# Hybrid decoder layer on one core: conditioning sums spread over the projections, convolution halos on ACT, attention paced anew

## The chip, the cores and the metric

The kernel runs on one core of a Trainium2 chip. The core has a matrix engine (PE), a vector engine (DVE), a scalar engine (ACT), a general engine (POOL) and a queue engine (SP) that here issues the DMAs; each works through its own list of instructions in order. The metric is the device time of one execution in microseconds (us).

## The reference, cut to what matters

One decoder layer over 2048 tokens of width 1024, all in float32:

```python
mod = silu(c) @ w_ada + b_ada            # (1, 6*1024)
sh1, sc1, ga1, sh2, sc2, ga2 = jnp.split(mod, 6, axis=-1)
h  = rms_norm(x, g_attn) * (1 + sc1) + sh1
x  = x + ga1 * hybrid_mixer(h, ...)      # h @ w_in, two attentions, @ w_out
h2 = rms_norm(x, g_mlp) * (1 + sc2) + sh2
u  = causal_dwconv(h2 @ w_up, conv_w, conv_b)   # width 3 along the tokens
a, g = jnp.split(u, 2, axis=-1)
x  = x + ga2 * ((silu(g) * a) @ w_down)
y  = rms_norm(x, g_final)
```

Eight heads use attention over a sliding window of 128 tokens, eight use "forgetting" attention over all earlier tokens. `w_ada` has 1024 x 6144 numbers (24 MB); `mod` is one row, made by a product of a vector with that matrix.

## The kernel before

**Blocks and stages.** The tokens are cut into four blocks of 512 (n = 0 to 3). For each block there are three generators. `s1(n)` is the input projection. `s2(n)` is the attention. `s3(n)` is the output projection ("out", `L1179`), the row statistics, the up-projection (44 column blocks `ci` of 128 rows, 24 matmuls each, `L1297`) with the convolution, and the down-projection (`L1179` again). Every matmul operand is split into a high and a low float32r part (`wh`, `wl`; `hh`, `hl`; `ph`, `pl`), the high by ACT (`L384`, `L115`, `L724`), the low by DVE (`L385`, `L530`, `L725`), and each product is three matmuls.

**What sets the order.** `merge(main, side, ratio)` takes one event after another of a main generator and between them steps of an attention generator, so that the attention keeps to `ratio` times the main work that is done; `RM` scales these ratios. The five merges at the end of the function pair: s1(1) and s1(2) with s2(0); s3(0) with s2(1); s1(3) and s3(1) with s2(2); s3(2) with s2(3); s3(3) runs alone. An event `("B", us)` of the main generator is a place where PE would be idle, and attention may run there without main work. A scheduler then moves instructions by priority, on each engine, where their operands allow; what results is a fixed list per engine.

**Attention.** `s2` works on units. A unit of forgetting attention has scores (`L964`), which ACT copies out with a bias (`L981`), a column maximum (`L989`, `L991`), its spreading over rows (`L996`, `L1003`), a subtraction on DVE (`L1010`, `L1014`), the exponential on ACT (`L1015`), sums (`L1025`, `L1035`), and for each group of columns the split `ph`, `pl` (`L724`, `L725`) and the products with v (`L1059`, `L1062`). `DEPTH` is the number of split groups that are held before the oldest one's products are issued, `PB` the number of buffers for `ph` and for `pl`.

**Conditioning.** `w_ada` comes in 12 chunks of 512 columns, each in 8 steps of 256 KB. A step is one DMA (`wada`) and one DVE instruction (`L205` for the first of a chunk, `L207` for the others) that adds a scaled piece to `acc`; PE then sums `acc` over the partitions (`L262`, `L215`, `L226`). Chunks 0 to 3, which s1(0) needs, are made at the start in `first_groups`, whose DVE order is as written. Chunks 4 to 11 come from the generator `prologue_later`: 4 and 5 give the gate of the first residual (it must be there before s3(0)), 6 to 9 shift and scale of the second norm (`mod` at `L219`, `scl` at `L350`), 10 and 11 the second gate. `woven` takes one step of it after every eighth event of s1(1) and s1(2), and what the first gate lacks at their end in one go. `s3(0)` takes one step per event of its output projection, then in a loop (`while "mod" not in late`) whatever is missing up to `scl`, and two steps per pair of column blocks after that.

**The turn from out to up.** When the output projection of s3(n) ends, DVE forms the residual rows (`L1254`, `L1255`), ACT squares and sums them (`L491`), POOL takes the root (`L495`, `L496`), DVE and ACT scale the halves (`L1262`, `L1263`), PE transposes (`L517`), ACT applies `mod` and `scl` (`L525`, tile `hraw`) and splits (`L115`), DVE forms `hl` (`L530`), and the first up matmul can run.

**The convolution.** For each column block ACT evicts the PSUM tile `d` with bias and the third tap (`L1327`), DVE adds the other two taps (`L1330`, `L1333`). The first two columns of a block need the last two of the block before: `halo`. In blocks 1 to 3 DVE adds it (`L1338`); in blocks 0 to 2 ACT (`L1340`, two columns) and DVE (`L1341`, one column) form the halo for the next.

Of the kernel before, what the change touches and what calls it, by code (L numbers as in the profile page):

```python
# [11 lines left out]
AF = mybir.ActivationFunctionType  # L12
ALU = mybir.AluOpType
# [5 lines left out]
TB = 512  # L19
# [6 lines left out]
EPS = 1e-6  # L26
BIG = 1e30
NT = 10
RM = [1.0, 1.1, 1.0, 1.2]
GAPS = [1.5, 1.5, 1.2, 1.5]  # L30
FG = 3
NW = 1 + (FG > 0)
# [1 line left out]
FK = 4  # L34
WS = 10
KEEP = (0, 1)
DEPTH = 2
PB = 3
SD = 1
AD = 0  # L40
HOOKS = (13, 17, 20)
# [30 lines left out]
def tile_decoder_layer(  # L72
# [169 lines left out]
    def first_groups():  # L242
        rows = ready.pop(0)
        xts = []
        for k in range(KT):
            if k % 4 == 2:
                ps = pa.tile([P, 512], F32, tag="o", name="o0")
            else:
                ps = side_ps()
            transposes(ps, rows, k)  # L250
            xt = ap.tile([P, TB], F32, tag="act", name="xt")
            nc.scalar.copy(xt, ps)
            xts.append(xt)
        hh, hl = {}, {}
        acc = [dense_ps() for _ in range(4)]
        for tag, bufs in (("s", 3), ("o", 1), ("s", 3))[:FG]:
            acc.append(pa.tile([P, 512], F32, tag=tag, name="acc0", bufs=bufs))

        def shape(i, a):
            ps = side_ps(4)  # L260
            for j in range(4):
                nc.tensor.matmul(  # L262
                    ps[:, j : j + 1], a[:, j * P : (j + 1) * P], ones[:, 0:1],
                    start=True, stop=True,
                )
            js, jc = slice(2 * i, 2 * i + 2), slice(KT + 2 * i, KT + 2 * i + 2)
            nc.vector.tensor_add(mod[:, js], ps[:, 0:2], bada[:, js])
            nc.vector.tensor_add(mod[:, jc], ps[:, 2:4], bada[:, jc])
            nc.vector.scalar_tensor_tensor(
                scl[:, js], mod[:, jc], 1.0, gat[:, js], ALU.add, ALU.mult  # L270
            )

        def products(k, sets):
            a = k % 2
            for m in sets:
                i = NW * (k // 2) + m
                feed(i + 3, i + 2)
                wh, wl = parts[i]
                for g in range(4 * m, min(4 * m + 4, len(acc))):
                    gs = slice((g - 4 * m) * P, (g - 4 * m + 1) * P)  # L280
                    for j, (l, r) in enumerate(((wh, hh), (wh, hl), (wl, hh))):
                        nc.tensor.matmul(  # L282
                            acc[g], l[:, a, gs], r[k],
                            start=(k == 0 and j == 0), stop=(k == KT - 1 and j == 2),
                        )
                if a == 1:
                    parts.pop(i)
                    flow["used"] += 1

        prev = None  # L290
        for i in range(5):
            sums = None
            if i < 4:
                sums = ap.tile([P, 512], F32, tag="act", name="acc")
            for k in range(KT):
                if i < 4:
                    ada_pair(i, k, sums)
                if i > 0 and k == 1:
                    shape(i - 1, prev)
                    if i > 1:  # L300
                        for m in range(1, NW):
                            products(2 * i - 4, [m])
                            products(2 * i - 3, [m])
                if i > 0 and k in (3, 5):
                    kk = 2 * (i - 1) + (k - 3) // 2
                    modulate_one(*h_pair(hh, hl, kk), xts[kk], kk, 0, 0)
                    if k == 5:
                        products(kk - 1, [0])
                        products(kk, [0])
            prev = sums  # L310
            if i == 0:
                feed(3, 2)
        for m in range(1, NW):
            products(KT - 2, [m])
            products(KT - 1, [m])
        small_loads()
        for g in range(4):
            store_group(acc[g], q_d[0], 512 + g * P, 0.125)
        for g in range(FG):
            store_group(acc[4 + g], k_d[0], P + g * P, 1.0)  # L320
        return hh, hl
# [33 lines left out]
    def woven(side, extra, every):  # L355
        for i, event in enumerate(side):
            yield event
            if i % every == every - 1:
                next(extra, None)
        while "gate" not in late:  # L360
            next(extra)
# [170 lines left out]
    def h_pair(hh, hl, k, name="h"):  # L532
        if k not in hh:
            hh[k] = hp.tile([P, TB], F32R, tag="hh", name=name + "h")
            hl[k] = hp.tile([P, TB], F32R, tag="hl", name=name + "l")
        return hh[k], hl[k]
# [691 lines left out]
    def s3(n, after=()):  # L1228
# [58 lines left out]
        for f in range(NF):  # L1287
            if f == NF - 1:
                got[0, 0] = get(0)
                got[0, 1] = get(1)  # L1290
            res = []
            ups = []

            def up(ps, w, k, hf, hn):
                c = slice(hf * TB // hn, (hf + 1) * TB // hn)
                for i, (a, b) in enumerate(((0, h2h), (0, h2l), (1, h2h))):
                    nc.tensor.matmul(  # L1297
                        ps[:, c], w[a][:, k, :], b[k][:, c],
                        start=(k == 0 and i == 0), stop=(k == KT - 1 and i == 2),
                    )  # L1300

            if f == 0:
                ws = [weights(), weights()]
                ups = [dense_ps(), dense_ps()]
                for hf in range(2):
                    for part in range(2):
                        for k in range(KT):
                            need(k + 2, hf)
                            if hf == 0 and part == 1:
                                need(k // 2, 1)  # L1310
                            up(ups[part], ws[part], k, hf, 2)
                            if k % 4 == 3:
                                yield 1.3
            for part in range(2):
                ci = part * NF + f
                if f > 0:
                    w = weights()
                    ps = dense_ps()
                    for k in range(KT):
                        up(ps, w, k, 0, 1)  # L1320
                        if k % 2 == 1:
                            yield 1.3
                else:
                    ps = ups[part]
                u = tp.tile([P, TB], F32, tag="u", name="u", bufs=3)
                c0, c1, c2 = (cw[t][:, ci : ci + 1] for t in range(3))
                nc.scalar.activation(  # L1327
                    u, ps, AF.Identity, bias=cb[:, ci : ci + 1], scale=c2
                )
                nc.vector.scalar_tensor_tensor(  # L1330
                    u[:, 1:], ps[:, : TB - 1], c1, u[:, 1:], ALU.mult, ALU.add
                )
                nc.vector.scalar_tensor_tensor(  # L1333
                    u[:, 2:], ps[:, : TB - 2], c0, u[:, 2:], ALU.mult, ALU.add
                )
                hl = halo[:, ci, :]
                if n > 0:
                    nc.vector.tensor_add(u[:, 0:2], u[:, 0:2], hl)  # L1338
                if n < NB - 1:
                    nc.scalar.activation(hl, ps[:, TB - 2 : TB], AF.Copy, scale=c0)  # L1340
                    nc.vector.scalar_tensor_tensor(  # L1341
                        hl[:, 0:1], ps[:, TB - 1 : TB], c1, hl[:, 0:1], ALU.mult, ALU.add
                    )
                res.append(u)
            a, g = res
            for _ in range(2):
                next(extra, None)
            e = tp.tile([P, TB], F32, tag="t", name="e")
            nc.scalar.activation(e, g, AF.Tanh, scale=0.5)
            nc.vector.tensor_mul(a, a, g)  # L1350
            act = ap.tile([P, TB], F32, tag="act", name="act")
            nc.vector.scalar_tensor_tensor(act, e, 1.0, a, ALU.add, ALU.mult)
            acts.append(act)
# [101 lines left out]
    def chain(*gens):  # L1455
        for g in gens:
            yield from g
# [32 lines left out]
    def att_cost(n):  # L1490
        return MRG * (44.0, 72.0, 97.0, 124.0)[n]
# [20 lines left out]
    gat = columns(None, KT, "gat", g_raw)  # L1512
    late["extra"] = prologue_later()
    merge(s1(0), prologue_late(), 1.0)
    merge(woven(chain(s1(1), s1(2)), late["extra"], 8), s2(0), RM[0] * att_cost(0) / 190.0)
    merge(s3(0, [lambda: prime(2)]), s2(1), RM[1] * att_cost(1) / 383.0)
    merge(chain(s1(3), s3(1, [lambda: yprep(2, 1), lambda: prime(3)])), s2(2), RM[2] * att_cost(2) / 478.0)
    merge(s3(2, [lambda: yprep(3, 1)]), s2(3), RM[3] * att_cost(3) / 383.0)
# [73 lines left out]
```

## Time and profile before

| what | value |
|---|---|
| median of 3 runs | 2646.96 us (2644.52 to 2648.71) |
| the profiled execution's own time | 2648.82 us, its span 2647.1 us |
| PE, DVE, ACT busy | 96%, 73%, 55% of the span |
| HBM traffic over the span | 221 GB/s |
| chain that ended last, by engine | PE 83%, DVE 6%, DMA 6%, ACT 2% |

Busy time of PE counts matmuls that overlap, so it hides short waits; how fast PE really goes is read from how many matmuls end in a stretch, and from the granted clock (`PEclk`, 1.00 is full). Views "by window" give, for a stretch from A to B, its length, then for each engine busy time and the number of instructions, the clock, the DMA share and rate. The view of groups gives for each line the count, busy time, mean duration in ns, and the engine's idle time just before with what ended it.

### The profile page before, as it was taken

Reading aid. Unit: us, or ns where it says so; the run is one execution under the profiler, and the core shown is the slowest. Engines: PE = TensorE matmul, PEld = TensorE weight load, DVE = VectorE, ACT = ScalarE, POOL = GpSimd, SP = SyncE. Lnnn points to the kernel's source line nnn. Section 1 sums busy time; section 2 is a strip of 40 time slices with the busy share of each in tenths; the row PEclk is TensorE's granted clock in tenths of the full one; section 3 lists DMA queues with packets and bytes.
Section 4 is the critical chain, followed back from the end, with each engine's and each line's share of the span. In section 5 each row is a group of like instructions: output and inputs, shape, how many; then the busy total and the mean of one; then the engine's idle time right before and its main releaser. Section 6 shows DMA issues by size and latency. Waiting matters only on the chain.

```text
span 2647.1 us, 38431 instructions
## 1 busy us (share of the span) xinstructions
PE 2541.4 (96%) x12852; PEld 2151.1 (81%) x12852; DVE 1926.8 (73%) x3837; ACT 1458.4 (55%) x3061; POOL 84.1 (3%) x171
## 2 busy tenths in 40 slices
PE   7999999799999999999999999999998999999998
PEld 5888888688887889878888878888886778888887
DVE  6468767899998668788888767878888787444433
ACT  4456665555667675575556665755555666412222
POOL 0001000100000010000000001000000000000000
PEclk9999999799999999999999999999998999999999
DMA  6967679576556976756666799555544477655564
GB/s 230 305 203 254 204 231 344 182 254 211 188 189 212 288 239 215 251 199 240 228 230 235 258 290 312 176 182 194 187 153 148 139 235 246 252 191 191 193 238 173
DMA packets 304770, 588.25 MB, mean 222 GB/s; under 512 B 32188, under 2 KB 137396, under 8 KB 304572
## 3 DMA queue, kind: packets, MB, share of 16 engines
q1 hardware_dynamic: 304572, 585.79, 66.3%
q8 instruction: 102, 1.67, 0.3%
q14 instruction: 96, 0.79, 0.1%
HBM read 440.95 MB, written 144.71 MB: 221 GB/s over the span
## 4 chain that ended last, share of the span: by engine, by line
PE 83%; DVE 6%; DMA 6%; ACT 2%; issue 1%; SPq 1%; POOL 0%; POOLq 0%; DVEq 0%; ACTq 0%
PE d L1297 36%; PE d L1179 21%; PE d L619 8%; PE s L964 4%; PE d L647 3%; PE o L1062 2%; PE o L1059 2%; DVE t L1010 1%; DMA wada<-in_w_ada_dram 1%; PE d L282 1%; DMA q<-qd 1%; PE s L794 1%; PE mb L996 1%; PE pt L836 1%; DVE pl L725 1%
## 5 line engine op out<-in xcount | busy, mean ns | idle before, releaser
L1297 PE MATMUL d<-hh,wkh 128*128 128x512 f32 (+1 forms) x920 | 351.3, 384 | 3.3 <-ACT hh L115 1.6
L1297 PE MATMUL d<-hl,wkh 128*128 128x512 f32 (+1 forms) x920 | 353.2, 385 | 0.1
L1297 PE MATMUL d<-hh,wkl 128*128 128x512 f32 (+1 forms) x920 | 351.7, 383 | 0.0
L384 ACT CAST wh<-wr 128x1024 fp32r<-128x1024 f32 (+5 forms) x184 | 188.7, 1027 | 162.4 <-PE d L1297 72.0
L385 DVE TENSOR_TENSOR wl<-wr,wh 128x1024 fp32r<-128x1024 f32 (+5 forms) x184 | 219.0, 1191 | 80.0 <-ACT wh L384 78.4
L981 ACT ACTIVATE t<-s,bc 128x256 f32<-128x256 f32 (+3 forms) x464 | 201.1, 483 | 124.7 <-PE s L964 70.6
L1327 ACT ACTIVATE u<-d,cb,cw 128x512 f32<-128x512 f32 x176 | 136.3, 778 | 192.9 <-PE d L1297 179.8
L1330 DVE SCALAR_TENSOR_TENSOR u<-d,cw,u 128x511 f32<-128x511 f32 x176 | 130.4, 743 | 153.6 <-ACT u L1327 152.8
L724 ACT CAST ph<-t 128x512 fp32r<-128x512 f32 (+2 forms) x304 | 177.1, 591 | 110.0 <-PE o L1059 109.6
L1297 PE MATMUL d<-hh,wh 128*128 128x512 f32 (+1 forms) x552 | 211.1, 385 | 0.4 <-ACT hh L115 0.4
L1297 PE MATMUL d<-hh,wl 128*128 128x512 f32 (+1 forms) x552 | 211.0, 383 | 0.2 <-DVE wl L385 0.2
L1297 PE MATMUL d<-hl,wh 128*128 128x512 f32 (+1 forms) x552 | 211.0, 383 | 0.0
L725 DVE TENSOR_TENSOR pl<-t,ph 128x512 fp32r<-128x512 f32 (+2 forms) x304 | 192.9, 645 | 24.7 <-ACT ph L724 24.5
L964 PE MATMUL s<-q,kkb 128*128 128x256 f32 (+2 forms) x1024 | 197.0, 311 | 14.0 <-ACT t L981 5.9
L1297 PEld LDWEIGHTS d<-hh,wkh 128*128 128x128 f32 x920 | 173.2, 189 | 35.4 <-DVE halo L1341 2.2
L1297 PEld LDWEIGHTS d<-hh,wkl 128*128 128x128 f32 x920 | 173.9, 189 | 31.5
L1297 PEld LDWEIGHTS d<-hl,wkh 128*128 128x128 f32 x920 | 173.9, 189 | 30.9 <-DVE hl L530 0.5
L1015 ACT ACTIVATE t<-t 128x512 f32<-128x512 f32 (+2 forms) x304 | 170.3, 603 | 11.6 <-DVE t L1014 8.5
L964 PEld LDWEIGHTS s<-q,kkb 128*128 128x128 f32 x1024 | 153.8, 197 | 26.8 <-ACT t L981 8.2
L1062 PE MATMUL o<-pl,vvb 128*128 128x256 f32 (+2 forms) x512 | 148.8, 310 | 18.2 <-DVE pl L725 18.0
L1059 PE MATMUL o<-ph,vvb 128*128 128x256 f32 (+2 forms) x512 | 151.5, 311 | 8.2 <-ACT ph L724 6.2
L619 PE MATMUL d<-hh,wh 128*128 128x512 f32 x360 | 142.5, 399 | 6.6 <-DVE lf L662 4.0
(233 smaller groups left out, 6061.9 us busy)
## 6 DMA issues: line engine op xcount, KB each, us to landing
wkh<-wsu SPq DMA_DIRECT2D x110, 512.0 KB, 3.3
wkl<-wsu SPq DMA_DIRECT2D x110, 512.0 KB, 4.2
wr<-in_w_up_dram SPq DMA_DIRECT2D x66, 512.0 KB, 5.4
wkh<-wsd SPq DMA_DIRECT2D x55, 512.0 KB, 4.0
wkl<-wsd SPq DMA_DIRECT2D x55, 512.0 KB, 4.2
wada<-in_w_ada_dram SPq DMA_DIRECT2D x96, 256.0 KB, 5.8
wr<-in_w_in_c_dram SPq DMA_DIRECT2D x45, 512.0 KB, 4.6
wsu<-wh SPq DMA_DIRECT2D x44, 512.0 KB, 2.9
```

Of the source, the lines that this page charges most:

```text
L384: nc.scalar.copy(wh, raw)
L385: nc.vector.tensor_sub(wl, raw, r32(wh))
L619: nc.tensor.matmul(ps, a[:, k, :], b[k], start=(k == 0 and i == 0), stop=(k == KT - 1 and i == 2),)
L724: nc.scalar.copy(ph[:, e0:], src[:, e0:])
L725: nc.vector.tensor_sub(pl[:, e0:], src[:, e0:], r32(ph[:, e0:]))
L964: nc.tensor.matmul(ps[:, o + low(c0) : o + w], st["kks"][kb // 4][:, (kb % 4) * P : (kb % 4 + 1) * P], qs[a][:, low(c0) : w], start=(a == ...
L981: nc.scalar.activation(tt[:, plain : o + w], ps[:, plain : o + w], AF.Identity, bias=bias(kb))
L1015: nc.scalar.activation(t1, t1, AF.Exp)
L1059: nc.tensor.matmul(po[:, c:], v, ph[:, o + c : o + w], start=(kb == 0), stop=False)
L1062: nc.tensor.matmul(po[:, c:], v, pl[:, o + c : o + w], start=False, stop=(kb == nkb - 1))
L1179: nc.tensor.matmul(acc[t], l[:, ts], r[:, k % 2, :], start=(i == 0 and l is ah and r is wh), stop=(i == n_k - 1 and l is al),)
L1297: nc.tensor.matmul(ps[:, c], w[a][:, k, :], b[k][:, c], start=(k == 0 and i == 0), stop=(k == KT - 1 and i == 2),)
```

## The change

It has five parts.

1. `woven` takes a step of the late conditioning chunks after every fourth event of s1(1) and s1(2), not every eighth.
2. `DEPTH` 2 to 3 and `PB` 3 to 4: one more split group is held before its products are issued.
3. `RM` from 1.0, 1.1, 1.0, 1.2 to 1.0, 1.0, 1.0, 1.08: the attention of blocks 1 and 3 is spread more thinly over its stage.
4. In the convolution the halo carries the bias. ACT evicts columns 2 to 511 of a block (blocks 1 to 3) and then columns 0 and 1 in an instruction each, with the halo as the bias; it forms the next halo in two instructions. The two DVE instructions go.
5. In `first_groups` the first chunk's shift and scale are applied, and the first products issued, at the end of the first round of the loop and no longer inside the second.

```diff
-RM = [1.0, 1.1, 1.0, 1.2]
+RM = [1.0, 1.0, 1.0, 1.08]
-DEPTH = 2
-PB = 3
+DEPTH = 3
+PB = 4
...
-                if i > 0 and k == 1:
+                if i > 1 and k == 1:
                     shape(i - 1, prev)
...
-                if i > 0 and k in (3, 5):
+                if i > 1 and k in (3, 5):
...
             if i == 0:
+                shape(0, sums)
                 feed(3, 2)
+                for kk in range(2):
+                    modulate_one(*h_pair(hh, hl, kk), xts[kk], kk, 0, 0)
+                for kk in range(2):
+                    products(kk, [0])
...
-                nc.scalar.activation(
-                    u, ps, AF.Identity, bias=cb[:, ci : ci + 1], scale=c2
-                )
+                hl = halo[:, ci, :]
+                bias = cb[:, ci : ci + 1]
+                f0 = 0 if n == 0 else 2
+                nc.scalar.activation(u[:, f0:], ps[:, f0:], AF.Identity, bias=bias, scale=c2)
+                for j in range(f0):
+                    nc.scalar.activation(
+                        u[:, j : j + 1], ps[:, j : j + 1], AF.Identity,
+                        bias=hl[:, j : j + 1], scale=c2,
+                    )
...
-                hl = halo[:, ci, :]
-                if n > 0:
-                    nc.vector.tensor_add(u[:, 0:2], u[:, 0:2], hl)
                 if n < NB - 1:
-                    nc.scalar.activation(hl, ps[:, TB - 2 : TB], AF.Copy, scale=c0)
-                    nc.vector.scalar_tensor_tensor(
-                        hl[:, 0:1], ps[:, TB - 1 : TB], c1, hl[:, 0:1], ALU.mult, ALU.add
+                    nc.scalar.activation(
+                        hl, ps[:, TB - 2 : TB], AF.Identity, bias=bias, scale=c0
+                    )
+                    nc.scalar.activation(
+                        hl[:, 0:1], ps[:, TB - 1 : TB], AF.Identity, bias=hl[:, 0:1], scale=c1
                     )
...
-    merge(woven(chain(s1(1), s1(2)), late["extra"], 8), s2(0), RM[0] * att_cost(0) / 190.0)
+    merge(woven(chain(s1(1), s1(2)), late["extra"], 4), s2(0), RM[0] * att_cost(0) / 190.0)
```

The change also moves instructions, since the scheduler orders them anew. In the listings below, a line number of the change is four higher than that of the same line before (nine higher from the convolution on).

DVE at the turn from out to up in s3(0), before: the last scaling of a row half (`L1262`), conditioning steps (`L207`), the large subtraction of an attention unit (`L1014`), then `mod` and `scl`, on which every `hraw` waits.

```order
L1262 TENSOR_SCALAR x1row<-x1row,rs 128x512
L207 SCALAR_TENSOR_TENSOR acc<-wada,cc,acc 128x512 x2
...
L1014 TENSOR_TENSOR t<-t,mm 128x512 x5
L1014 TENSOR_TENSOR t<-t,mm 128x384
L1014 TENSOR_TENSOR t<-t,mm 128x256 x2
L207 SCALAR_TENSOR_TENSOR acc<-wada,cc,acc 128x512
L219 TENSOR_TENSOR mod<-sd,bada 128x16
L1022 TENSOR_TENSOR acc<-t 128x512
L725 TENSOR_TENSOR pl<-t,ph 128x512 x3
L350 SCALAR_TENSOR_TENSOR scl<-mod,gml 128x8
```

The same place in the change: `scl` stands ahead of the first scaling, and between the last scaling and the first `hl` there is one weight split.

```order
L354 SCALAR_TENSOR_TENSOR scl<-mod,gml 128x8
L207 SCALAR_TENSOR_TENSOR acc<-wada,cc,acc 128x512
L1266 TENSOR_SCALAR x1row<-x1row,rs 128x512
...
L207 SCALAR_TENSOR_TENSOR acc<-wada,cc,acc 128x512 x2
L951 TENSOR_TENSOR mx<-mx,t 128x384
L1029 TENSOR_TENSOR acc<-acc,t 128x256
L1266 TENSOR_SCALAR x1row<-x1row,rs 128x512
L389 TENSOR_TENSOR wl<-wr,wh 128x1024
L534 TENSOR_TENSOR hl<-hraw,hh 128x256 x2
```

Of the 64 late conditioning steps, 17 stand on DVE ahead of the last group store of s1(2) before, 34 in the change.

PE in the up-projection of s3(2), at a change of attention unit late in that stage, before: the maximum (`mt`), its spreading (`mb`), the row sums (`lt`), 16 score matmuls and a product with v stand together, with one up matmul among them.

```order
L989 MATMUL mt<-ident,mx 128x128 x2
L964 MATMUL s<-q,kkb 128x256 x4
L1297 MATMUL d<-hh,wkl 128x512
L996 MATMUL mb<-ident,m 128x128 x2
L964 MATMUL s<-q,kkb 128x256 x4
L1035 MATMUL lt<-ident,acc 128x128 x2
L964 MATMUL s<-q,kkb 128x256 x8
L1059 MATMUL o<-ph,vvb 128x256
L1297 MATMUL d<-hh,wkh 128x512
```

The same unit in the change: between `mt` and `mb` stand 13 up matmuls, and more follow after `lt`.

```order
L993 MATMUL mt<-ident,mx 128x128 x2
L968 MATMUL s<-q,kkb 128x256 x4
L1301 MATMUL d<-hh,wkl 128x512
L1301 MATMUL d<-hh,wkh 128x512
...
L1301 MATMUL d<-hh,wkl 128x512
L1000 MATMUL mb<-ident,m 128x128 x2
L968 MATMUL s<-q,kkb 128x256 x4
L1039 MATMUL lt<-ident,acc 128x128 x2
L1301 MATMUL d<-hh,wkh 128x512
L1301 MATMUL d<-hl,wkh 128x512
```

ACT in the up-projection of s3(1), two column blocks, before: an eviction, one halo instruction, and attention work around them.

```order
L1327 ACTIVATE u<-d,cb,cw_1148 128x512
L724 CAST ph<-t 128x512
L981 ACTIVATE t<-s,bc 128x256 x2
L1340 ACTIVATE halo<-d,cw_1128 128x2
L1327 ACTIVATE u<-d,cb,cw_1148 128x512
L724 CAST ph<-t 128x512
L981 ACTIVATE t<-s,bc 128x128
L1340 ACTIVATE halo<-d,cw_1128 128x2
L1349 ACTIVATE e<-u 128x512
```

The same in the change: each eviction is followed by two one-column instructions, each halo by a second one.

```order
L1334 ACTIVATE u<-d,cb,cw_1148 128x510
L1336 ACTIVATE u<-d,halo,cw_1148 128x1 x2
L1347 ACTIVATE halo<-d,cb,cw_1128 128x2
L1358 ACTIVATE e<-u 128x512
L1350 ACTIVATE halo<-d,halo,cw_1138 128x1
L388 CAST wh<-wr 128x1024
L1334 ACTIVATE u<-d,cb,cw_1148 128x510
L1336 ACTIVATE u<-d,halo,cw_1148 128x1 x2
```

In both, `halo` waits for DVE, since DVE reads the same PSUM tile before it.

More of the change, by code (lines that the diff above doesn't have):

```diff
@@ L297, in first_groups @@
                     ada_pair(i, k, sums)
-                if i > 0 and k == 1:
+                if i > 1 and k == 1:
                     shape(i - 1, prev)
[L300 to L303, printed above, removed]
-                if i > 0 and k in (3, 5):
+                    for m in range(1, NW):
+                        products(2 * i - 4, [m])
+                        products(2 * i - 3, [m])
+                if i > 1 and k in (3, 5):
                     kk = 2 * (i - 1) + (k - 3) // 2
```

## The prediction

> **What bounds the kernel now.** I read the page first, then busy time by window, then the waits of PE and DVE, and the timeline where PE stands.
>
> ```profile
> span 2647.1 us, 38431 instructions
> PE 2541.4 (96%) x12852; PEld 2151.1 (81%) x12852; DVE 1926.8 (73%) x3837; ACT 1458.4 (55%) x3061; POOL 84.1 (3%) x171
> PEclk9999999799999999999999999999998999999999
> ```
>
> PE is the bound nearly everywhere, so only time in which PE stands, or runs at a low clock, can be won. Its full speed is read from the last block, where it runs alone, and from short runs of the chain that ended last:
>
> ```profile
> 2288.14 230.72 PE d L1297 x1026
> 384.11 0.44 PE pt L836 x4
> 384.55 0.48 PE s L794 x4
> ```
>
> That is 230.72/1026 = 0.225 us for a 512-wide matmul, 0.12 for a 256-wide and 0.11 for a 128-wide one. Against these, the windows show where PE falls behind.
>
> ```profile
> 467.50:506.10 38.60, 22.03 (x83) 15.81 (x82) 38.14 (x74) 20.68 (x43) 9.05 (x9) 0.58 0.72 250
> 804.50:811.10 6.60, 3.39 (x14) 2.53 (x13) 6.60 (x14) 6.58 (x16) 0.00 (x0) 0.79 0.69 184
> 1915.10:1923.70 8.60, 3.25 (x18) 2.26 (x17) 8.56 (x17) 8.60 (x20) 0.00 (x0) 0.84 0.62 212
> 1983.80:1997.10 13.30, 6.91 (x40) 6.16 (x39) 13.18 (x26) 12.58 (x28) 0.00 (x0) 0.74 0.43 138
> 2130.40:2135.00 4.60, 3.22 (x25) 2.81 (x23) 4.06 (x9) 1.98 (x5) 0.00 (x0) 1.00 0.80 273
> 2164.00:2173.40 9.40, 6.13 (x42) 4.81 (x40) 7.57 (x20) 8.04 (x20) 0.00 (x0) 1.00 0.70 219
> 100.00:400.00 300.00, 290.83 (x1602) 253.92 (x1601) 210.48 (x517) 191.00 (x427) 18.64 (x41) 0.99 0.76 238
> 506.10:820.00 313.90, 310.68 (x1480) 258.63 (x1481) 282.54 (x517) 193.03 (x366) 1.39 (x6) 0.99 0.59 197
> 1700.00:1900.00 200.00, 199.81 (x1049) 170.33 (x1047) 168.09 (x340) 111.35 (x242) 1.03 (x5) 1.00 0.56 191
> ```
>
> The first row is the turn from out to up in s3(0): 83 matmuls in 38.6 us, DVE busy without a gap (38.14), the clock at 0.58. It is the largest hole after the start. The third to sixth rows are the first, second, seventh and last of eight stretches in s3(2) with s2(3) where attention matmuls stand together and wait for ACT and DVE. From 506 to 820 and from 1700 to 1900 PE loses next to nothing.
>
> **The sum, part by part.** It is made against the profiled execution, 2648.8 us, which is 1.9 above the median shown.
>
> *Conditioning at the turn.* DVE's groups in the window, its timeline there, and then ACT's and PE's:
>
> ```profile
> L207 DVE SCALAR_TENSOR_TENSOR acc<-wada,cc,acc 128x512 f32<-128x512 f32 x15 | 10.7, 742 | 0.0
> L205 DVE TENSOR_SCALAR acc<-wada,cc 128x512 f32<-128x512 f32 x2 | 1.0, 480 | 0.0
> ...
> 486.50 0.49 DVE L1262 TENSOR_SCALAR x1row<-x1row,rs 128x512 f32<-128x512 f32 x1 [0.46 <-POOL rs L496]
> 500.94 0.74 DVE L207 SCALAR_TENSOR_TENSOR acc<-wada,cc,acc 128x512 f32<-128x512 f32 x1
> 501.60 0.17 DVE L219 TENSOR_TENSOR mod<-sd,bada 128x16 f32<-128x16 f32 x1
> 504.09 0.16 DVE L350 SCALAR_TENSOR_TENSOR scl<-mod,gml 128x8 f32<-128x8 f32 x1
> ```
>
> ```profile
> 504.28 1.47 ACT L525 ACTIVATE hraw<-d,mod,scl 128x256 f32<-128x256 f32 x3
> ...
> 506.11 0.58 PE L1297 MATMUL d<-hh,wh 128*128 128x256 f32 x1 [0.45 <-ACT hh L115]
> ```
>
> The rows of the residual are scaled by 486.5 + 0.5 = 487.0, but `hraw` starts at 504.28, since `scl` is last: 17.3 us in which only the conditioning and attention run. In the change's order 17 of those steps have gone into s1(1) and s1(2), `scl` stands ahead of the first scaling, and one weight split lies between the last scaling and the first `hl`. Ahead of the last scaling DVE has six steps in the change, five before, so I take it to end as late as now, and the hole to be 17.3 us shorter. PE's work between 489 and 506 must then run later: 11 score matmuls (2.5 us) and 28 small ones at up to 0.11 each, about 4.3 us together. Net 13 us. If the rows end later because attention crowds DVE there, it may be nothing; if relieved DMAs and DVE bring them earlier, 20.
>
> *The price of that.* The 17 steps now run in s1(1) and s1(2). DVE there:
>
> ```profile
> DVE acc L207 <- DMA wada<-in_w_ada_dram: 28.7, 12, 5.8
> DVE acc L205 <- DMA wada<-in_w_ada_dram: 7.1, 3, 4.1
> ```
>
> ```profile
> PE d L619 <- DVE lf L662: 4.0, 1, 4.0
> ...
> 362.83 4.35 DMA wada<-in_w_ada_dram
> ```
>
> (Between 75 and 400 us; the last row is from the chain that ended last.) Fifteen of the steps there waited 35.8 us for their load, 2.4 us each, at the head of DVE's queue, with attention's `pl`, the weight splits `wl` and the gates `lf` behind. PE lost 4.0 us to `lf` just after such a wait: 11%. Seventeen more steps make 41 us of waiting, and 11% of it is 4.5. DVE is busy 210 of 300 us, so the steps' own 12.5 us fit in. As any new order may also dissolve the one stall of 4.0, I take 3 of loss, between 4 of gain and 20 of loss (half of the 41).
>
> *DEPTH, PB and RM.* PE's waits from 1900 to 2240:
>
> ```profile
> PE o L1062 <- DVE pl L725: 10.6, 11, 3.7
> PE o L1059 <- ACT ph L724: 6.2, 4, 3.2
> ```
>
> The products with v wait 16.8 us. By count times 0.12, the eight stretches lose 8.60 - 18 x 0.12 = 6.4, 13.30 - 40 x 0.12 = 8.5, and so on to 9.40 - 42 x 0.12 = 4.4; together 39. In the change's order the first is pulled apart by up matmuls and the second is in three pieces, 6.4 and about 5 won; but the stretch at 2130 (25 matmuls, lost 1.6) becomes one of 54, as the one at 2057 is now, which loses 5.2: 4 lost. Net 7 of gain. Nothing says that DVE keeps pace, 84% busy from 1700 to 1900 (168.09 of 200), so the ends are 20 of gain and 10 of loss. In s3(0) the stretch at 804.5 (6.60 us for 14 matmuls, 4.9 lost) has no run of that length left in the new order: 4 of gain, at least 0. At the end of s3(2) a run of 16 products and transposes now stands last, with no main work behind it in the stage: 1 lost.
>
> *The halo on ACT.*
>
> ```profile
> L1338 DVE TENSOR_TENSOR u<-u,halo 128x2 f32<-128x2 f32 x132 | 19.7, 149 | 0.0
> L1341 DVE SCALAR_TENSOR_TENSOR halo<-d,cw,halo 128x1 f32<-128x1 f32 x132 | 27.3, 208 | 2.6 <-ACT halo L1340 2.6
> L1340 ACT ACTIVATE halo<-d,cw 128x2 f32<-128x2 f32 x132 | 34.5, 261 | 84.6 <-DVE u L1338 56.0 <-DVE u L1333 28.2
> ```
>
> DVE loses 264 instructions, 47.0 us. ACT gains 264 + 132 = 396; none of one column exists before, the nearest row takes 0.261 us, so 103 us over four stages. In s3(1) and s3(2) that is 132 x 0.261 = 34 us on ACT, which is 56% busy (111.35 of 200), and 44 x 0.357 = 16 less on DVE. The wait of 84.6 us stays for the most part: the change's `halo` still waits for DVE's last reading of the tile (block 0 has that wait already, 28.2), and the second halo instruction needs the result of the first. PE's cover is the up-projection itself, 24 matmuls or 5.4 us per column block. I take 1 lost; the ends are 3 won, if DVE is the late one, and 6 lost, if ACT is. The Trainium skill ("ScalarE: Activation LUTs", Rules for kernel authors) speaks against the move: it tells to use VectorE and not ScalarE for adds and multiplies, and budgets about 0.3 us for each ACTIVATE; by that ACT would gain about 119 us (an estimate), which no row here shows.
>
> *The start.*
>
> ```profile
> 23.10 0.15 DVE L267 TENSOR_TENSOR mod<-sd,bada 128x2 f32<-128x2 f32 x1
> 23.61 1.52 ACT L525 ACTIVATE hraw<-xt,mod,scl 128x512 f32<-128x512 f32 x2 [2.06 <-DVE scl L269]
> 25.70 2.07 PE L282 MATMUL d<-hh,wh 128*128 128x512 f32 x4 [3.99 <-ACT hh L115]
> ```
>
> `mod` no longer waits behind two weight splits and two steps, and comes 1.4 us earlier; but a weight cast now stands between `hraw` and `hh` on ACT, and the second chunk's steps all come after. 0.5 won, from 2 won to 2 lost.
>
> Sum: 13 + 7 + 4 + 0.5 won, 3 + 1 + 1 lost: 19.5. 2648.8 - 19.5 = 2629.3, and 1.9 less for the median: 2627. The bounds taken at once would reach 2594 and 2686; not all fall one way, so the forecast's own range is 2612 to 2640.
>
> **The rivals.** *The turn doesn't shrink.* DVE has no gap from 467.5 to 506.1, so the steps may only have filled time in which attention would run, and the rows end later. For it: 38.14 of 38.6. Against: 17.3 us after the rows end, with `scl` alone missing. Then the 13 fall to about 0: 2640.
>
> *ACT becomes late.* The one-column instructions stand ahead of `ph` and `t` on ACT. If the 34 us reach PE from 1900 on, where ACT fills 8.60 of 8.60 us at 1915, a third of them, 11: 2638. This is how the rule of the Trainium skill ("ScalarE: Activation LUTs", Rules for kernel authors) would come out. Block 1, with PE at full clock and ACT half idle, speaks against it.
>
> *The loads block DVE (slower).* If conditioning steps wait 41 us at the head of DVE's queue in s1 and PE has no other work, the share that arrives decides: from 55% (22.5 us, instead of the 3 taken) the sum is no gain, and at all of it 2627 + 38 = 2665. For it: the chain passes through `wada` and the DMA share is 0.76. Against: 11% arrived so far.
>
> *The change doesn't do what it says.* The pacing may not pace: in the built order the attention of s2(3) ends at the same place, by a flush. Without the 7 and the 4 it is 2638.
>
> A difference under 0.2%, 5.3 us, can't be told from none. Forecast 0.60; no shorter turn 0.10; ACT late 0.08; loads block 0.12; no pacing 0.10. The three middle cases lie just under 2641.7 (2647 less 5.3), so a part of them counts as no change: faster 0.75, same 0.13, slower 0.12. The range 2604 to 2654 reaches to the middle cases and into the slower one.
>
> **What would show it.** In the changed profile: the first up matmul of s3(0) about 17 us earlier after the end of out, with a clock above 0.58; more `wada` waits of DVE before 400, near 70 us, and some 4 us more of PE's waits on what DVE held up there; 396 more ACT instructions of about 0.2 to 0.26 us; PE's waits for `pl` and `ph` after 1900 under 10; no hole near 1915. The prediction is wrong if the turn is still over 30 us, if PE stands in s1 for 20 us more, or if ACT is what PE waits for in s3(2).

## The result, and the profile after

The changed kernel takes 2628.22 us (median of 4 runs, 2624.52 to 2630.82); four runs of the kernel before in the same comparison have a median of 2647.84 us. The ratio is 0.9922, with a 95% interval from 0.9905 to 0.9939: 20.7 us faster, give or take 4.5. The profiled execution took 2628.70 us, 20.1 less than that of before.

From the page, after: the span, the busy times, and the granted clock in 40 slices.

```profile
span 2627.0 us, 38614 instructions
PE 2532.2 (96%) x12852; PEld 2142.8 (82%) x12852; DVE 1898.2 (72%) x3573; ACT 1561.8 (59%) x3457; POOL 85.8 (3%) x171
PEclk8999999999999999999999999999999999999999
```

ACT is busy 103.4 us more (1561.8 against 1458.4), DVE 28.6 less. The place to look is PE's own progress. Its rows in the trace give the start of the first matmul of each stage; two of them, after (before, the same two were at 415.54 and 506.11):

```profile
426.08 0.39 PE L1183 MATMUL d<-wh,yh 128*128 128x512 f32 x1
495.90 0.58 PE L1301 MATMUL d<-hh,wh 128*128 128x256 f32 x1 [1.74 <-ACT hh L115]
```

From such rows the span can be cut into stretches. Each number below is the start of a stage less the start of the one ahead of it; all later traces are cut in the same way, and each is one execution.

| stretch (us) | before | after | difference |
|---|---|---|---|
| start to the first input matmul | 25.7 | 24.5 | -1.2 |
| inputs, s1(0) to s1(2) | 389.8 | 401.6 | +11.8 |
| turn: first out to first up of s3(0) | 90.6 | 69.8 | -20.8 |
| up and down of s3(0) | 454.9 | 457.6 | +2.7 |
| s1(3), s3(1), out of s3(2) | 708.9 | 704.8 | -4.1 |
| up and down of s3(2), out of s3(3) | 604.6 | 596.1 | -8.5 |
| the rest of s3(3) | 372.6 | 372.6 | 0.0 |

The windows of after that answer to those shown of before: the end of the turn, the old hole at 1915, a stretch where attention still stands together, and s1.

```profile
480.80:495.90 15.10, 7.74 (x32) 5.56 (x30) 14.64 (x33) 11.04 (x25) 8.63 (x8) 0.78 1.01 366
1915.10:1923.70 8.60, 8.60 (x55) 7.74 (x55) 7.82 (x15) 3.39 (x8) 0.21 (x1) 1.00 0.52 163
2032.60:2047.10 14.50, 9.45 (x56) 8.26 (x54) 14.50 (x28) 11.65 (x27) 0.20 (x1) 0.88 0.47 145
100.00:400.00 300.00, 285.41 (x1560) 247.52 (x1559) 209.97 (x503) 181.70 (x407) 18.95 (x40) 0.98 0.74 237
```

The turn's hole is 15.1 us and 32 matmuls, where it was 38.6 us and 83. At 1915 PE is full, with 55 matmuls where 18 ran. But from 100 to 400 PE is busy 5.4 us less than before (285.41 against 290.83), and 42 matmuls fewer are done.

Why the hole shrank is read from DVE's and ACT's rows there.

```profile
488.29 0.17 DVE L354 SCALAR_TENSOR_TENSOR scl<-mod,gml 128x8 f32<-128x8 f32 x1
...
491.90 0.49 DVE L1266 TENSOR_SCALAR x1row<-x1row,rs 128x512 f32<-128x512 f32 x1 [0.46 <-POOL rs L500]
```

```profile
493.46 0.56 ACT L529 ACTIVATE hraw<-d,mod,scl 128x256 f32<-128x256 f32 x1
```

`scl` is ready before the rows are scaled, and `hraw` follows the last scaling (491.90 + 0.49) by 1.1 us, where it followed by 17.3.

The dearest single place of what s1 paid begins at 258 us. First DVE, where a conditioning step waits for its load, with the reciprocal's sum `rl` and the gate `lf` behind it, then PE, where first the scores and then the next input matmuls wait.

```profile
261.31 0.75 DVE L207 SCALAR_TENSOR_TENSOR acc<-wada,cc,acc 128x512 f32<-128x512 f32 x1 [3.72 <-DMA wada<-in_w_ada_dram]
...
263.30 0.68 DVE L1044 TENSOR_REDUCE rl<-lt 128x4 f32<-128x512 f32 x1
...
264.76 0.18 DVE L676 SCALAR_TENSOR_TENSOR lf<-lf,na 128x32 f32<-128x32 f32 x1
```

```profile
264.04 1.22 PE L968 MATMUL s<-q,kkb 128*128 128x256 f32 x4 [5.79 <-DVE rl L1044]
...
266.44 0.63 PE L623 MATMUL d<-hl,wh 128*128 128x512 f32 x1
266.87 0.63 PE L623 MATMUL d<-hh,wl 128*128 128x512 f32 x1
```

PE stands 5.79 us, and is slow afterwards: the two rows are 0.43 us apart, not 0.225. The window shows the clock that was granted:

```profile
264.00:270.30 6.30, 6.26 (x19) 5.27 (x20) 6.06 (x19) 3.92 (x10) 0.56 (x1) 0.50 0.81 249
```

PE was busy for 6.26 of these 6.30 us at half the clock, so the wait cost its own length and about 3 us more. The Trainium skill ("TensorE: Matmul & The Clock Gate", What's actually happening) states that PE falls to half rate after at least one idle window of about 3.4 us and returns after at least one busy window of the same length. The half rate agrees with 0.43 us; the return took 6.3 us or a little more here, nearly two of the page's windows.

DVE's waits for the conditioning loads from 75 to 400 us in all, after (before: 28.7 and 7.1 us):

```profile
DVE acc L207 <- DMA wada<-in_w_ada_dram: 46.4, 21, 6.2
DVE acc L205 <- DMA wada<-in_w_ada_dram: 2.2, 2, 1.2
```

### The profile page after: what moved, and what is told of

Read it like the earlier page. It is cut to its first block, busy times and chain, and to the rows that moved or that the text cites. A ratio compares the mean times of both kernels' runs of the same rounds, so it can differ in the third digit from the quotient of the medians.

```text
span 2627.0 us, 38614 instructions
## 1 busy us (share of the span) xinstructions
PE 2532.2 (96%) x12852; PEld 2142.8 (82%) x12852; DVE 1898.2 (72%) x3573; ACT 1561.8 (59%) x3457; POOL 85.8 (3%) x171
## 3 DMA queue, kind: packets, MB, share of 16 engines
q1 hardware_dynamic: 304572, 585.79, 66.2%
## 4 chain that ended last, share of the span: by engine, by line
PE 83%; DVE 5%; DMA 5%; ACT 4%; issue 1%; SPq 1%; POOL 1%; POOLq 0%; ACTq 0%; DVEq 0%
PE d L1301 36%; PE d L1183 22%; PE d L623 7%; PE s L968 4%; PE d L651 2%; PE o L1066 2%; PE o L1063 2%; DVE t L1014 1%; PE d L282 1%; DMA zrow<-zd 1%; DVE pl L729 1%; PE mb L1000 1%; DMA wada<-in_w_ada_dram 1%; PE s L798 1%; ACT hraw L529 1%
## 5 line engine op out<-in xcount | busy, mean ns | idle before, releaser
L1334 ACT ACTIVATE u<-d,cb,cw 128x510 f32<-128x510 f32 (+1 forms) x176 | 136.9, 778 | 166.6 <-issue 89.3
L968 PE MATMUL s<-q,kkb 128*128 128x256 f32 (+2 forms) x1024 | 191.1, 305 | 11.9 <-DVE rl L1044 5.8
```

What stands on the lines that cost most here:

```text
L968: nc.tensor.matmul(ps[:, o + low(c0) : o + w], st["kks"][kb // 4][:, (kb % 4) * P : (kb % 4 + 1) * P], qs[a][:, low(c0) : w], start=(a == ...
```

## The experiments

Each kernel was timed beside the kernel before; differences in us are the ratio's difference from 1, or from the 0.9922 of the changed kernel, times 2648. Against the changed kernel they carry an uncertainty of 5 to 6 us, since its own interval enters.

### Each part alone

The steps alone:

```diff
-    merge(woven(chain(s1(1), s1(2)), late["extra"], 8), s2(0), RM[0] * att_cost(0) / 190.0)
+    merge(woven(chain(s1(1), s1(2)), late["extra"], 4), s2(0), RM[0] * att_cost(0) / 190.0)
```

> The kernel before with a conditioning step after every fourth event of s1(1) and s1(2), nothing else. Theory (the turn carries the gain): the stretch at the turn from out to up in s3(0) falls from 39 us to about 15 and PE stands some 13 to 15 us less there, while s1 costs 4 to 8 us; the time is 6 to 11 us below the kernel before. Rival (the waits for loads eat it): s1 gives back 13 or more and the time is the same or higher. Rival (the gain needs the other parts): the turn stays over 30 us.

The halo alone (and the two DVE instructions go):

```diff
+                nc.scalar.activation(u[:, f0:], ps[:, f0:], AF.Identity, bias=bias, scale=c2)
+                for j in range(f0):
...
-                    nc.vector.tensor_add(u[:, 0:2], u[:, 0:2], hl)
...
+                        hl[:, 0:1], ps[:, TB - 1 : TB], AF.Identity, bias=hl[:, 0:1], scale=c1
```

> The kernel before with the halo columns on ACT, nothing else. Theory (both engines have room): within 3 us of the kernel before, up or down, although ACT is busy some 100 us more. Rival (ACT becomes late, as the Trainium skill's rule on adds and multiplies in "ScalarE: Activation LUTs", Rules for kernel authors, would have it): 6 to 11 us slower, with PE's waits on ACT's ph in s3(2) grown. Second rival (DVE was the late one in s3(2)): 3 to 8 us faster, with PE's waits on DVE's pl fallen.

The pacing alone:

```diff
-RM = [1.0, 1.1, 1.0, 1.2]
+RM = [1.0, 1.0, 1.0, 1.08]
...
-DEPTH = 2
-PB = 3
+DEPTH = 3
+PB = 4
```

> The kernel before with the new RM, DEPTH and PB, nothing else. Theory (the attention of s2(3) is spread and the products wait less for pl and ph): 7 to 11 us faster, all of it after 1800 us and at the stretch near 804. Rival (nothing is paced, the attention ends at the same place by a flush, and the fall of the waits for pl in the changed kernel came from the halo on ACT): within 3 us of the kernel before, and PE's wait for pl after 1900 us stays at 8 to 12 us.

The first conditioning groups alone:

```diff
-                if i > 0 and k == 1:
+                if i > 1 and k == 1:
...
             if i == 0:
+                shape(0, sums)
                 feed(3, 2)
+                for kk in range(2):
+                    modulate_one(*h_pair(hh, hl, kk), xts[kk], kk, 0, 0)
+                for kk in range(2):
+                    products(kk, [0])
```

> The kernel before with the new order of the first conditioning groups, nothing else. Theory: 0 to 2 us faster, since mod is ready 1.4 us earlier but a weight cast stands between hraw and hh on ACT. Rival (the later chunks' steps, now behind the first products, come later and so does the first input projection): 1 to 3 us slower, with the first full projection matmul later.

| alone | median (us) | ratio to before, 95% | difference |
|---|---|---|---|
| steps | 2663.16 | 1.0054 (1.0038 to 1.0070) | +14.3 |
| halo | 2644.37 | 0.9979 (0.9968 to 0.9990) | -5.6 |
| pacing | 2639.31 | 0.9964 (0.9953 to 0.9976) | -9.5 |
| first groups | 2660.60 | 1.0041 (1.0025 to 1.0057) | +10.9 |

They sum to +10, where all together are -20.7. The pacing's time is in the range that I expected. By place it isn't: in its trace, which is 6.3 us shorter than that of before, 4.3 are won in s3(2), 3.1 in the inputs and 2.3 from s1(3) to out of s3(2), the turn loses 2.6, and s3(0) gains nothing. The halo's 5.6 is outside the 3 us of my theory and in the range of the second rival, with DVE the late one. The steps and the first groups came out slower where I expected them faster. For the first groups the rival isn't right either: 10.9 is more than its 1 to 3 us, and the first input matmul comes earlier, not later. For the steps the rival's time came true, but not its reason: s1 gave back 12.7 us, near the 13 that it names, and the turn won 24.4, a gain up to there. Three windows of that kernel:

```profile
484.40:494.60 10.20, 4.45 (x21) 3.06 (x19) 9.36 (x20) 8.22 (x19) 4.92 (x5) 0.82 1.05 361
1183.60:1188.10 4.50, 0.89 (x8) 0.65 (x6) 4.50 (x9) 3.34 (x7) 0.00 (x0) 0.90 1.00 394
2066.30:2083.40 17.10, 10.84 (x63) 9.61 (x61) 16.26 (x30) 13.20 (x29) 0.20 (x1) 0.80 0.26 78
```

The hole at the turn is 10.2 us, smaller still than in the changed kernel. The loss comes behind it: 10.2 in up and down of s3(0), 9.6 from s1(3) to out of s3(2), and 5.9 in s3(2). About half of the 10.2 is the part's own price: 34 matmuls more run in s3(0) than in the kernel before (2189 for 2155), attention that has left the turn, some 5 us. The last two rows above show two of its places; here are the same two in the kernel with the first groups alone, whose edit lies in the first 55 us.

```profile
1188.20:1192.70 4.50, 0.88 (x8) 0.63 (x6) 4.50 (x10) 3.40 (x7) 0.00 (x0) 1.00 0.98 382
2065.10:2082.20 17.10, 11.04 (x64) 9.82 (x62) 16.31 (x30) 13.25 (x30) 0.21 (x1) 0.80 0.29 86
```

And the same in the kernel before:

```profile
1183.00:1188.00 5.00, 5.00 (x26) 3.91 (x25) 5.00 (x13) 3.35 (x8) 0.00 (x0) 1.00 1.00 401
2057.00:2068.80 11.80, 8.79 (x55) 8.08 (x53) 11.80 (x22) 9.70 (x23) 0.20 (x1) 0.86 0.37 120
```

In both kernels PE does 8 matmuls in 4.5 us between 1183 and 1193 us where before it does 26 in 5.0, and later they have a stretch of 63 or 64 matmuls in 17.1 us where before it is 55 in 11.8. Neither edit is near. The mechanism of the first place is plain in DVE's rows. The kernel with the first groups alone:

```profile
1186.95 3.70 DVE L1014 TENSOR_TENSOR t<-t,mm 128x512 f32<-128x512 f32 x6
1190.56 0.75 DVE L1337 SCALAR_TENSOR_TENSOR u<-d,cw,u 128x510 f32<-128x510 f32 x1
...
1192.42 0.22 DVE L1345 SCALAR_TENSOR_TENSOR halo<-d,cw,halo 128x1 f32<-128x1 f32 x1
```

The kernel before:

```profile
1185.09 0.21 DVE L1341 SCALAR_TENSOR_TENSOR halo<-d,cw,halo 128x1 f32<-128x1 f32 x1
...
1186.07 3.69 DVE L1010 TENSOR_TENSOR t<-t,mm 128x512 f32<-128x512 f32 x6
```

The same six subtractions of an attention unit, 3.7 us, stand ahead of the convolution of a column block in the one and behind it in the other. PE needs the PSUM tile that `halo` reads last:

```profile
PE d L1301 <- DVE halo L1345: 3.6, 1, 3.6
```

A small edit early in the program gave a new order everywhere behind it, and this order had a few such places. The first groups' own effect was what I had forecast (the first input matmul at 25.2 and not 25.7); what their time measured was the order.

### Each part left out

One part undone in the changed kernel, in the same way: 8 for 4 in `woven`; the halo of before; `first_groups` of before; `RM`, `DEPTH` and `PB` of before.

```diff
-    merge(woven(chain(s1(1), s1(2)), late["extra"], 4), s2(0), RM[0] * att_cost(0) / 190.0)
+    merge(woven(chain(s1(1), s1(2)), late["extra"], 8), s2(0), RM[0] * att_cost(0) / 190.0)
```

> The changed kernel with a conditioning step after every eighth event again; the other four parts stay. Its order of PE is that of the changed kernel from the up-projection of s3(0) on (9225 of 12808 matmuls alike at the end), so this is the part by itself. Theory (own effect: the turn shrinks by more than s1 loses, and the 14 us that the part cost alone came from a new order far behind it): 5 to 12 us slower than the changed kernel, that is 8 to 15 us faster than the kernel before; the turn is back at about 40 us, and PE reaches the end of s1(2)'s matmuls some 15 us earlier. Rival (the part costs wherever it is put): some 14 us faster than the changed kernel.

```diff
-                        hl[:, 0:1], ps[:, TB - 1 : TB], AF.Identity, bias=hl[:, 0:1], scale=c1
+                    nc.vector.scalar_tensor_tensor(
+                        hl[:, 0:1], ps[:, TB - 1 : TB], c1, hl[:, 0:1], ALU.mult, ALU.add
```

> The changed kernel with the halo as before (132 instructions on ACT, 264 on DVE). Theory (DVE is the later of the two engines, ACT has room): 1 to 6 us slower than the changed kernel, with more of PE's waits on DVE's pl from 1900 us on. Rival (ACT is what PE waits for, by the Trainium skill's rule in "ScalarE: Activation LUTs", Rules for kernel authors): 3 us or more faster than the changed kernel. Second rival (only the new order counted when it was tried alone): within 3 us either way, with no shift of waits between ph and pl.

```diff
-                if i > 1 and k == 1:
+                if i > 0 and k == 1:
```

> The changed kernel with the first conditioning groups in the order of before. Theory (its own effect is what shows at the start, 0.6 to 1.4 us; the 12 us that the part cost alone came from new orders behind 250 us that the new pacing doesn't have): within 3 us of the changed kernel. Rival (the part costs by itself): 9 to 15 us faster than the changed kernel.

```diff
-RM = [1.0, 1.0, 1.0, 1.08]
+RM = [1.0, 1.1, 1.0, 1.2]
...
-DEPTH = 3
-PB = 4
+DEPTH = 2
+PB = 3
```

> The changed kernel with RM, DEPTH and PB of before. Theory (the pacing is worth what it was alone, and it is also what keeps the other parts' new orders harmless): 15 to 28 us slower than the changed kernel, at or above the kernel before. Rival (the parts add up, and the pacing is worth the 9.5 us that it brought alone): 8 to 11 us slower than the changed kernel.

And half of the pacing undone:

```diff
-DEPTH = 3
-PB = 4
+DEPTH = 2
+PB = 3
```

> The changed kernel with DEPTH 2 and PB 3 again; RM stays as changed. Theory (the third held split group carries what the pacing is worth, since PE's products then wait less for pl and ph everywhere): 10 to 20 us slower than the changed kernel, with PE's waits for pl and ph over the whole program grown by as much. Rival (RM carries it, by spreading the attention): within 4 us of the changed kernel.

| left out | median (us) | ratio to before, 95% | against the changed kernel |
|---|---|---|---|
| steps | 2632.75 | 0.9933 (0.9918 to 0.9949) | +2.9 |
| halo | 2631.78 | 0.9927 (0.9913 to 0.9942) | +1.3 |
| first groups | 2634.95 | 0.9939 (0.9927 to 0.9952) | +4.5 |
| pacing | 2650.53 | 1.0000 (0.9991 to 1.0009) | +20.7 |
| DEPTH and PB | 2641.59 | 0.9971 (0.9958 to 0.9983) | +13.0 |

Without the pacing nothing of the gain is left; each of the other three can go for less than can be told from nothing. So these times neither confirm nor refute my 5 to 12 us for the steps, 1 to 6 for the halo and at most 3 for the first groups, nor the rival that the halo on ACT costs 3. The first groups, +10.9 alone, are a gain of 4.5 here if anything: the rival that the part costs by itself falls, as does that for the steps.

The kernel without the steps is the cleanest test of the turn, since PE's order is that of the changed kernel from 760 us on, late in the up-projection of s3(0). Its windows of the turn and of what follows, up to the first down matmul:

```profile
465.80:507.30 41.50, 23.28 (x90) 16.98 (x88) 40.33 (x77) 21.00 (x44) 9.41 (x9) 0.60 0.71 253
507.30:796.60 289.30, 289.30 (x1382) 242.12 (x1383) 252.80 (x415) 186.75 (x354) 1.02 (x5) 0.99 0.58 199
```

The hole is back, 41.5 us. By stretches, against the changed kernel: the turn 92.0 for 69.8 (22.2 longer), the inputs 389.6 for 401.6 (12.0 shorter), up and down of s3(0) 452.0 for 457.6 (5.6 shorter; 25 matmuls fewer run there, 2151 for 2176, all of them attention that ran in the turn, some 4 us), later stretches 4.6 shorter, the start 1.1 longer: in all 1.1 longer. The steps move about 22 us out of the turn and pay 12 of them in s1 and 6 in s3(0): 4 are left.

Without `DEPTH` and `PB` the loss is in s1 (4.3 longer) and from s1(3) to out of s3(2) (5.1 longer); s3(2) itself is 1.1 longer. Its rows show one place each: a stretch in s1, and PE's longest wait from s1(3) on (the same kind of wait is 1.6 and 0.6 us there in the changed kernel).

```profile
384.90:394.30 9.40, 2.55 (x14) 1.62 (x13) 8.28 (x22) 6.43 (x18) 0.00 (x0) 0.84 0.88 281
```

```profile
PE mb L1000 <- ACT t L1019: 5.2, 1, 5.2
```

Neither is a wait for `pl` or `ph`, which I had expected: over the whole program the waits of the products with v for those fell from 24.2 us before to 10.6 after, and are 15.8 here, 5 of the 13 us. Going on to the old `RM` (no pacing at all) adds 6.5 in s3(0) and 4.5 in s3(2), where I had looked for it.

### A new order on purpose

The same meaningless edit in both kernels:

```diff
-RM = [1.0, 1.1, 1.0, 1.2]
+RM = [1.01, 1.1, 1.0, 1.2]
```

> The kernel before with the first number of RM 1.01 and not 1.0: no purpose but another order from the middle of s1(1) on. Theory (a new order by itself moves this kernel by as much as the parts that were tried alone): 3 to 14 us from the kernel before, most likely above it. Rival (the order is not what moved those kernels): within 3 us.

```diff
-RM = [1.0, 1.0, 1.0, 1.08]
+RM = [1.01, 1.0, 1.0, 1.08]
```

> The changed kernel with the first number of RM 1.01 and not 1.0: no purpose but another order from the middle of s1(1) on. Theory (with the new pacing the attention of s3 is cut into runs that don't depend on how the order before them fell): within 5 us of the changed kernel. Rival (the changed kernel owes its time to a lucky order): 6 us or more slower than it.

The kernel before so edited takes 2657.05 us, ratio 1.0028 (1.0014 to 1.0042), 7.4 slower than before. It has the two places again:

```profile
1180.30:1184.80 4.50, 0.88 (x8) 0.64 (x6) 4.50 (x9) 3.35 (x7) 0.00 (x0) 1.00 1.01 401
2057.20:2074.30 17.10, 11.10 (x63) 10.04 (x61) 16.24 (x30) 13.32 (x29) 0.20 (x1) 0.80 0.26 79
```

The changed kernel so edited takes 2638.85 us, ratio 0.9966 (0.9951 to 0.9981): 11.7 slower than the changed kernel, still 9.0 faster than before. Beside the kernel before with the same edit it is 16.4 faster, give or take 5.4. My theory that the new pacing makes the kernel indifferent to the order falls; the rival holds. Its traced execution lost 5.8 us more in the inputs, 3.6 in s3(0) and 8.5 in s3(2), but took 2647.22 us, 8.4 over its median, so these can't be taken at their size.

### Loads two steps ahead

```diff
+        ws = []
+        for k in range(KT + WAH):
+            if k < KT:
+                w = ap.tile([P, 512], F32, tag="act", name="wada")
+                with behind():
+                    nc.sync.dma_start(w, w_ada[i, k])
+                ws.append(w)
+            if k >= WAH:
+                ada_step(acc, ws[k - WAH], k - WAH)
+                yield
```

> The changed kernel with the late conditioning pieces loaded two steps ahead of the step that uses them; nothing is left out. Theory (what s1 lost to the 17 added steps is DVE standing at their loads, with lf and rl behind it): DVE's waits for wada before 480 us fall from 53 us to under 25, PE reaches the end of s1(2) 5 to 12 us earlier, and the time is 3 to 12 us under the changed kernel. Rival (s1 lost the time to attention that DVE and ACT can't serve faster, or to the new order): the waits fall but the time stays within 3 us of the changed kernel or rises.

2631.87 us, ratio 0.9930 (0.9913 to 0.9947): 2.1 from the changed kernel, no difference that can be told. The edit didn't reach its aim, waits under 25 us. DVE's waits from 75 to 400 us:

```profile
DVE acc L212 <- DMA wada<-in_w_ada_dram: 40.5, 19, 4.5
DVE acc L210 <- DMA wada<-in_w_ada_dram: 5.0, 2, 3.3
```

They fell by 3 us only, since the scheduler brought the steps forward with their loads: between 240 and 330 us the median from a load's issue to its step is 4.4 us in the changed kernel and 5.4 here. The inputs are 7.2 us shorter all the same, the turn 4.0 and s3(2) 7.7 longer. The stall of 5.8 us is gone: at its place PE keeps the full clock.

```profile
255.90:262.70 6.80, 4.04 (x28) 3.32 (x26) 5.63 (x15) 5.39 (x11) 1.39 (x4) 1.00 0.79 253
```

Whether steps that don't wait would give s1 its 12 us back was not tried and stays open.

## Why the prediction was right in its number, and where not

*By place.* The turn won 20.8 for the 17.3 of the sum, the start 1.2 for 0.5, and s3(2) 8.5 for 6; from s1(3) to out of s3(2) 4.1 were won, where the sum had no term. s3(0) lost 2.7, where the sum has 4 won and 4.3 lost. s1 lost 11.8 for 3. So one place cost 9 us more than forecast, and the others together gave 9 more. That 2627 stands so near 2628.22 is luck.

*The turn: mechanism right.* `scl` was what `hraw` waited for, and 22.2 us went in the clean comparison. The attention that then ran later is 25 matmuls, some 4 us, near the 4.3 of the sum; the rates given with that term come to more, 2.5 + 28 x 0.11 = 5.6, and 16 of the 28 small matmuls were sums of the conditioning and not attention.

*The price in s1: the step that failed.* It said that 41 us of new waits for loads come and that 11% of them reach PE, 3 us. The inputs grew by 11.8. The waits grew by 12.8 us only (48.6 for 35.8), and the loss doesn't follow their sum. With the steps alone the inputs grew by 12.7, and DVE's waits from 75 to 400 us were 35.0, no more than before:

```profile
DVE acc L207 <- DMA wada<-in_w_ada_dram: 32.0, 18, 6.5
DVE acc L205 <- DMA wada<-in_w_ada_dram: 3.0, 2, 2.2
```

With the loads two steps ahead the waits fell by 3.1 and the inputs by 7.2. In the changed kernel most of the loss is one stall, 5.8 us and about 3 more at half clock, and it stands behind a load's wait of 3.7. So what counts is where a wait falls and not a share of all waits; and I costed a stall at its length, though a PE that has stood 5.79 us then runs 6.3 us at half clock. What makes s1 longer in the other orders with the early steps is not shown. The stated bounds, 4 of gain to 20 of loss, held it. The rival that the loads block DVE named the place, at half the 22.5 us from which it decides.

*DEPTH, PB and RM: right in s3(2), blind elsewhere.* The hole at 1915 went, and PE's longest waits for `pl` after 1900 are now these (8.5 with `ph`, 16.8 before); the second row is in the same answer:

```profile
PE o L1066 <- DVE pl L729: 8.3, 8, 2.5
...
PE d L1301 <- ACT halo L1350: 0.8, 1, 0.8
```

But left out, the part costs 20.7 us, not the 10 that the sum gives it (7 and 4 won, 1 lost), and most of what `DEPTH` and `PB` bring lies in s1 and from s1(3) to s3(2), where the sum had no term. There one wait of PE, just ahead of the up-projection of s3(1), sorts all fourteen traces: 5.2 us in the seven with `DEPTH` 2, and 1.6 in the seven with `DEPTH` 3. Here are before and after:

```profile
PE mb L996 <- ACT t L1015: 5.2, 1, 5.2
```

```profile
PE mb L1000 <- ACT ph L728: 1.6, 1, 1.6
```

With it goes the stretch from s1(3) to out of s3(2): 708.9 to 718.5 us in those seven, 703.2 to 706.6 in these. So this gain is not one of the order. The gain in s3(2) is less sure: 593.0 to 604.6 us in the seven traces with the whole pacing, 600.0 to 610.5 in the six with none of it. The rival "no pacing" is refuted.

*The stretch at 804: given back.* The hole is gone, but s3(0) has not gained the 4 us: among others, PE now waits 4.7 us for `al` at 931.8, where before that wait was 1.9.

*The halo: right that it costs nothing.* The durations were off:

```profile
L1336 ACT ACTIVATE u<-d,halo,cw 128x1 f32<-128x1 f32 x264 | 78.2, 352 | 0.0
L1347 ACT ACTIVATE halo<-d,cb,cw 128x2 f32<-128x2 f32 x132 | 47.3, 358 | 60.8 <-DVE u L1343 59.6 <-DVE rl L1048 0.9
L1350 ACT ACTIVATE halo<-d,halo,cw 128x1 f32<-128x1 f32 x132 | 47.2, 358 | 1.7
```

One column takes 0.352 to 0.358 us, not 0.261. The row I went by was the wrong neighbour: with the same two columns, the halo was a copy with a scale and took 0.261, and is now an identity with a bias operand as well and takes 0.358. ACT's busy time grew by the 103 forecast all the same, since neighbours overlap (264 x 0.352 is 92.9 us, and the row's busy time 78.2): two errors that cancel. Alone the part gained 5.6 us, and left out it cost 1.3; neither is more than a new order can do. So the rule of the Trainium skill ("ScalarE: Activation LUTs", Rules for kernel authors) that adds and multiplies go to VectorE does not decide here; its budget of about 0.3 us for an ACTIVATE is a little under what these took. The order on each engine counts for more. On DVE `halo` could get behind 3.7 us of subtractions, and in the six traces with it there PE waits 1.5 to 11.5 us for it; in the eight with it on ACT, 0.8 to 4.4. ACT isn't free of such places. Without the pacing PE has this one:

```profile
PE d L1301 <- ACT halo L1350: 3.6, 1, 3.6
```

*What the prediction had no rival for.* Each part re-sorts the whole program, and a re-sorting alone moved the time by 7.4 and by 11.7 us. So the time of one kernel doesn't tell what a part is worth, and the sum over parts tried alone has the wrong sign. By cause, then, the account was not shown right; by place it held for the turn and, in this order, for s3(2).

The stages of all fourteen traces, which have nearly as many orders, tell more, though each is one execution. With the steps at every fourth event (eight traces) the turn takes 66.2 to 73.8 us, the inputs 394.4 to 407.3 and s3(0) 457.3 to 465.1; at every eighth (six traces) it is 90.6 to 94.2, 385.0 to 393.0 and 450.9 to 455.3. By the means 22.7 us are won, and 12.8 and 7.1 are paid: some 3 us of gain, where the sum had 10. The pacing wins by the means 7.9 us from s1(3) to out of s3(2) (`DEPTH` 3 against 2) and 6.4 in s3(2), and with the early steps s3(0) takes 457.3 to 461.2 us under the new `RM` and 463.9 and 465.1 under the old. So most of the 20.7 us is the pacing. What part of that is its work in any order, and what the luck of this one, stays open; the edit of 1% takes 11.7 of the 20.7, give or take 6, but with that edit on both sides 16.4 are left. No version tried here beats the changed kernel.

## What to carry to other kernels

Where a scheduler re-sorts the program, time a meaningless edit before you assign a few us to a meaningful one, and leave a part out of the whole as well as trying it alone. Read a gain by place: cut the trace at the first matmul of each stage, and see which stretch changed and whether the edit can reach it. Work moved out of a hole is paid where it lands, and a wait at the head of an engine's queue can cost what stands behind it.

## What the runs showed of the hardware that I had not expected

After a wait of 5.79 us PE's 512-wide matmuls came 0.43 us apart, at a granted clock of 0.50 for 6.3 us or a little more after the wait's end. That is about 3 us of lost work, so the stall cost some 50% above its length. And for a small ACT instruction out of PSUM the kind counted and not the width: 0.358 us for two columns with a bias, 0.352 and 0.358 for one, 0.261 for two without a bias. The kind is a copy there and an identity here, so the rows don't part the function from the bias.
